# Attention outputs stored as half-precision pairs and turned by the reads of the last stage

## The chip, the cores and the metric

The kernel runs on one core of a Trainium2 chip. The core has a matrix engine (TensorE, PE in the rows), a vector engine (VectorE, DVE), an engine for activation functions and scaled copies (ScalarE, ACT), a general engine (GpSimd, POOL) and SyncE (SP), whose queue issues nearly all DMA transfers of this kernel. The engines run side by side, each through its own instructions in their order, and wait for each other on semaphores. The metric is the device time of one execution in microseconds (us), lower is better. Before the change it is 2896.48 us, the median of 3 runs from 2891.53 to 2901.36.

## What is computed

Two layers on 2048 tokens of width 1024: a Mamba-2 mixer, then multi-head latent attention with 16 heads, and a final RMS norm. The change lies in the end of the second layer, where `causal_block_attention` returns one 64-wide output per token and head:

```python
def mla_mixer(h, k_nope, k_rope, v, cos, sin, w_in, g_q, w_uq, w_out):
    ...
    o = causal_block_attention(q_nope, q_rope, k_nope, k_rope, v)
    o = o.reshape(Bsz, S, MLA_HEADS * V_HEAD) * jax.nn.silu(gate)
    return o @ w_out

h = h + mla_mixer(...)
return rms_norm(h, g_final)
```

## The kernel before

The program has three parts: `layers` (the Mamba layer and the projections for attention, up to about 1960 us), `attention` (to about 2705 us) and `back` (to the end). Results that cross the parts lie in device memory, among them the attention outputs `o_d` and the gates `gate_d`, both with 1024 channels as rows and 2048 tokens as columns.

**Attention.** A job is one head and one block of 512 queries (16 heads, 4 blocks, 64 jobs). Scores are made with keys on the partitions, two key tiles of 128 at a time (a duo); ACT takes the exponential into `x` (line 1371) and copies it to half precision as the high part of `PTs` (line 1376), POOL or DVE subtracts to get the low part (`lows`, line 1389), and PE multiplies the pair with the values (lines 1404 to 1406). The results of a job lie in one PSUM tile `o`, with queries on the partitions: [128, 4 tiles, 64 channels, and the row sum]. Row maxima for later jobs are taken by DVE from extra score products (lines 1252 and 1254), turned, stored in `m_d` and read back as rows (lines 1261 to 1270). On PE the order is the order of the code (`manual_schedule`); on the other engines and in SP's queue a scheduler orders by its own estimates.

When a job's last product is done, `finish` divides by the row sums: a reciprocal (line 1420) and a product into one half of the pair tile `Op` (line 1423), which holds two heads. After the odd head, three duos later (`TURN`), `store` has PE turn the four [128 queries, 128 channels] tiles into a score bank (line 1433), ACT copies the bank to `Os` (line 1435), and SP stores it in `o_d` (line 1437): 32 stores of 256 KB. The stores of heads 12 and 13 also start loads of the output weights (`load_wo`).

**Back.** The output projection runs over 4 blocks of 512 tokens, with 8 k-tiles of 128 channels each. `gated` makes the left operand of a k-tile: SP reads `o_d` into `os` and the gate beside it (lines 1519, 1520), DVE multiplies the two and a factor per channel (line 1521), and `split` makes a pair for float32 products (ACT line 107, DVE line 108). PE then runs 24 products per k-tile (`mm3`, lines 84 to 86). In the first block the loop goes k-tile by k-tile over 8 banks. Its k-tiles 0 and 1 are called early: they lie in `xT` buffers of a pool that lives through attention, so that their reads and products may run while attention still does. The others lie in a pool `bsp`, which opens when attention's pool `asp` closes; `os` has three buffers and the pairs `oT` have nine.

Of the kernel before, what the change touches and what calls it, by code (L numbers as in the profile page):

```python
# [10 lines left out]
F32 = mybir.dt.float32  # L11
F32R = mybir.dt.float32r
BF16 = mybir.dt.bfloat16
F16 = mybir.dt.float16
I32 = mybir.dt.int32
AF = mybir.ActivationFunctionType
ALU = mybir.AluOpType
# [50 lines left out]
class Net:  # L68
# [400 lines left out]
    def value_weights(self, owed):  # L469

        nc, v = self.nc, self.nc.vector
        for n in range(2):
            cs = slice(1024 + n * 512, 1536 + n * 512)
            raw = [self.t(self.wp, "wraw", [P, TB], bufs=WRAW) for _ in range(2)]
            for k in range(2):
                nc.sync.dma_start(raw[k], self.a["kv_w_up"][k * P:(k + 1) * P, cs])
            if owed:
                nc.sync.dma_start(*owed.pop())
            yield
            u = [self.t(self.wp, "wraw", [P, TB], F32R, bufs=WRAW) for _ in range(2)]  # L480
            for k in range(2):
                nc.scalar.activation(u[k], raw[k], AF.Abs, scale=self.gkl[:, k:k + 1])
            yield
            ps = self.t(self.pp, "tr", [P, TB], bufs=4)
            for k in range(2):
                nc.tensor.matmul(ps, self.ones_r, u[k], start=k == 0, stop=k == 1)
            x = self.t(self.sp, "cacc", [P, TB], bufs=2)
            v.tensor_scalar(x, ps, TINY, None, ALU.max)

            e = self.t(self.sp, "craw", [P, TB], I32, bufs=3)  # L490
            v.tensor_scalar(e, x.bitcast(I32), 23, None, ALU.logical_shift_right)
            f = self.t(self.sp, "cacc", [P, TB], I32, bufs=2)
            v.tensor_scalar(f, e, -1, 264, ALU.mult, ALU.add)
            v.tensor_scalar(f, f, 23, None, ALU.logical_shift_left)
            v.tensor_scalar(e[0:1], e[0:1], -25, None, ALU.add)
            v.tensor_scalar(e[0:1], e[0:1], 23, None, ALU.logical_shift_left)
            v.tensor_scalar(e[0:1].bitcast(F32), e[0:1].bitcast(F32), self.gdown[0:1], None, ALU.mult)
            nc.sync.dma_start(self.us_d[n * 512:(n + 1) * 512], e[0:1, :].bitcast(F32))
            for k in range(2):
                nc.gpsimd.tensor_tensor(raw[k], raw[k], f.bitcast(F32), ALU.mult)  # L500
            yield
            for k in range(2):
                w = self.t(self.wp, "wraw", [P, 2, TB], F16, bufs=WRAW)
                self.pair16(w[:, 0], w[:, 1], raw[k], self.gklv[:, k:k + 1])
                owed.append((self.wu_d[2 + n][k], w))
                yield
                nc.sync.dma_start(*owed.pop())
# [669 lines left out]
    def open_heads(self):  # L1177
# [9 lines left out]
        for i in range(2):  # L1187
            at = 2 * T + T // P * 130
            Q = self.quer[0, i] = kv[i][0:98, at:at + 2 * TB].rearrange("p (s t) -> p s t", s=2)
            self.fill_q(Q, 0, i)  # L1190
            nc.gpsimd.memset(self.keys[i][96:98, 0, :], MSCALE)
            nc.gpsimd.memset(self.vals[i][:, :, 128:130], 2.0 ** -14)
        self.load_k(0, 0, NB - 1)

    def load_vq(self):
# [109 lines left out]
    def heads(self, sp):  # L1305
# [109 lines left out]
        def finish(n):  # L1415

            h, qb = jobs[n]
            O = outs.pop(n)
            ri = self.t(sp, "ri", [P, 4], bufs=2)
            v.reciprocal(ri, O[:, :, 64])  # L1420
            if (h // 2, qb) not in pairs:
                pairs[h // 2, qb] = self.t(sp, "Op", [P, 4, 2, 64], bufs=6)
            v.tensor_tensor(pairs[h // 2, qb][:, :, h % 2, :], O[:, :, 0:64],
                            ri.unsqueeze(2).to_broadcast([P, 4, 64]), ALU.mult)
            if h % 2:
                later.append((step[0] + TURN, lambda: store(h, qb)))

        def store(h, qb):

            op = pairs.pop((h // 2, qb))  # L1430
            ps = bank()
            for j in range(4):
                nc.tensor.transpose(ps[:, j * P:(j + 1) * P], op[:, j].rearrange("p h d -> p (h d)"), self.ident)
            o = self.t(sp, "Os", [P, TB], bufs=2)
            act(o, ps, AF.Copy)
            r0 = (h // 2) * P
            done = nc.sync.dma_start(self.o_d[r0:r0 + P, qb * TB:(qb + 1) * TB], o)
            if h == NH - 3:
                with self.tc.issue_after(done.ins):
                    self.load_wo(qb)  # L1440
# [47 lines left out]
    def back(self):  # L1488
        nc, a, v, hp = self.nc, self.a, self.nc.vector, self.hp
        with ExitStack() as ctx:  # L1490
# [19 lines left out]
            def gated(b, k):  # L1510
# [5 lines left out]
                else:  # L1516
                    s = self.t(sp, "os", [P, 2, TB], bufs=3)
                o, gt = s[:, 0], s[:, 1]
                nc.sync.dma_start(o, self.o_d[rows, ts])
                nc.sync.dma_start(gt, self.gate_d[rows, ts])  # L1520
                v.scalar_tensor_tensor(o, o, us[:, k:k + 1], gt, ALU.mult, ALU.mult)
                u = self.t(self.xq, "xT", [P, 2, TB], F32R, bufs=8) if early else \
                    self.t(sp, "oT", [P, 2, TB], F32R, bufs=9)
# [76 lines left out]
    def run(self):  # L1600
        tc = self.tc
        with ExitStack() as whole:
# [5 lines left out]
            self.constants(cp)  # L1608
            self.h_d = dp.tile([T, D], F32, name="h_d")
            self.gate_d = dp.tile([D, T], F32, name="gate_d")  # L1610
            self.o_d = dp.tile([D, T], F32, name="o_d")
            self.xp_d = [dp.tile([TB, 2 * D], F16, name=f"xp{b}_d") for b in range(2 * NB)]
            self.m_d = dp.tile([NH * NB, P, 32], F16, name="m_d")
            self.qn_d = dp.tile([1024, 2, T], F16, name="qn_d")
# [70 lines left out]
```

## Time and profile before

The profiled execution took 2894.94 us, of which the span from the first to the last instruction is 2893.2 us.

| | us |
|---|---|
| median of 3 runs | 2896.48 |
| profiled execution | 2894.94 |
| its span | 2893.2 |
| PE busy in the span | 2809.5 (97%) |
| DVE, ACT, POOL busy | 2105.2, 1826.1, 854.8 |
| last product of attention starts at | 2704.05 |
| first product of `back` starts at | 2705.40 |

How to read it: the page lists busy time by engine, the busy shares in 40 slices, the chain of work that ended last (followed back from the last instruction, at each step to what released it), and groups of instructions with their mean durations and the idle time before them. Other views of the trace give the instructions in order of time, the waits by who waited for whom, and busy times by stretch. A row `x<-s` names the tile written and the tiles read. Products on PE overlap, so the distance from one start to the next is what one costs, and is less than the duration shown.

### The profile page before, as it was taken

To read this page: it belongs to the slowest core of one execution; us is meant where nothing else is said; L and a number is where in the kernel's file an instruction comes from. 1 tells how busy PE (TensorE), PEld (TensorE's weight loads), DVE (VectorE), ACT (ScalarE), POOL (GpSimd) and SP (SyncE) were. 2 spreads that over 40 slices of the span, in tenths; PEclk is the share of its full clock that TensorE was granted. 3 is DMA by queue.
4 is the path that set the end of the run, shared out by engine and by line. 5 is a ranking of instruction groups with operands and counts; after the bars stand their busy time and mean duration, and the time that the engine had idled before them with its cause. 6 is when DMAs were issued, how large, how long until landed. Compare 5 with 4: busy or idle time off the path is not lost.

```text
span 2893.2 us, 58394 instructions
## 1 busy us (share of the span) xinstructions
PE 2809.5 (97%) x21358; PEld 1643.2 (57%) x21358; DVE 2105.2 (73%) x5123; ACT 1826.1 (63%) x3948; POOL 854.8 (30%) x984
## 2 busy tenths in 40 slices
PE   7899999999999999999999999999999999999998
PEld 3455556554555555454555545545666666665787
DVE  7789987887777878779776455357777777778454
ACT  8777655666666766556554434234888888888522
POOL 0221221111222211222211122223666665665200
PEclk9999999999999999999999999999999999999999
DMA  9765736456464566636646877761222222223453
GB/s 294 248 208 193 215 118 215 149 171 192 146 237 132 176 192 218 212 117 214 209 138 233 252 227 230 235 206 59 72 55 63 64 51 74 67 64 89 166 198 109
DMA packets 308068, 470.77 MB, mean 163 GB/s; under 512 B 129474, under 2 KB 171234, under 8 KB 306340
## 3 DMA queue, kind: packets, MB, share of 16 engines
q1 hardware_dynamic: 296644, 431.11, 47.7%
q0 software_dynamic: 11136, 35.92, 3.4%
q8 instruction: 168, 2.75, 0.4%
q14 instruction: 120, 0.98, 0.1%
HBM read 332.83 MB, written 119.41 MB: 156 GB/s over the span
## 4 chain that ended last, share of the span: by engine, by line
PE 68%; DVE 16%; DMA 6%; ACT 5%; issue 4%; SPq 1%; POOL 1%; DVEq 0%; ACTq 0%; POOLq 0%
PE mm L84 11%; PE mm L85 11%; PE mm L86 11%; PE s L1365 4%; PE s L1366 4%; PE s L1367 4%; PE s L1252 4%; PE tr L85 3%; PE tr L84 3%; PE tr L86 3%; DVE cacc L647 3%; PE o L1405 2%; PE o L1406 2%; PE o L1404 2%; DMA big<-cumT 2%
## 5 line engine op out<-in xcount | busy, mean ns | idle before, releaser
L1389 POOL TENSOR_TENSOR PTs<-x,PTs 128x512 f16<-128x512 f32 (+1 forms) x380 | 439.2, 1179 | 264.6 <-ACT PTs L1376 173.6
L1371 ACT ACTIVATE x<-s 128x512 f32<-128x512 f32 (+3 forms) x640 | 326.9, 524 | 53.7 <-PE s L1367 34.6
L84 PE MATMUL mm<-xT,wsp 128*128 128x512 f16 x800 | 305.4, 382 | 6.1 <-ACT wsp L115 4.9
L85 PE MATMUL mm<-xT,wsp 128*128 128x512 f16 x800 | 304.9, 381 | 0.0
L86 PE MATMUL mm<-xT,wsp 128*128 128x512 f16 x800 | 304.4, 381 | 0.0
L1376 ACT ACTIVATE PTs<-x 128x1024 f16<-128x1024 f32 (+1 forms) x320 | 297.2, 929 | 9.4
L1254 DVE CUSTOM_DVE_ANT_0 junk<-s,fence,mx 128x512 bf16<-128x512 f32 (+1 forms) x372 | 242.1, 651 | 43.9 <-PE s L1252 3.8
L1406 PE MATMUL o<-K,PTs 128*128 128x65 f16 x2176 | 262.4, 192 | 2.0 <-POOL PTs L1389 1.5
L1404 PE MATMUL o<-K,PTs 128*128 128x64 f16 x2176 | 263.7, 192 | 0.1
L1405 PE MATMUL o<-K,PTs 128*128 128x65 f16 x2176 | 263.4, 194 | 0.0
L837 POOL TENSOR_TENSOR Xp<-Xw,Xp 128x512 fp32r<-128x512 f32 x64 | 90.5, 1414 | 504.1 <-ACT Xp L836 325.2
L1404 PEld LDWEIGHTS <-PTs 128*128 128x128 f16 x2176 | 204.6, 97 | 52.1 <-issue 4.3
L84 PE MATMUL mm<-wsp,xT 128*128 128x512 f16 (+1 forms) x640 | 230.5, 362 | 3.6 <-ACT craw L641 3.6
L85 PE MATMUL mm<-wsp,xT 128*128 128x512 f16 (+1 forms) x640 | 231.2, 361 | 2.1 <-DVE wsp L116 2.1
L1405 PEld LDWEIGHTS <-PTs 128*128 128x128 f16 x2176 | 202.7, 97 | 53.4 <-issue 1.0
L647 DVE SCALAR_TENSOR_TENSOR cacc<-craw,pack,cacc 128x512 f32<-128x512 f32 x288 | 215.5, 777 | 23.7 <-ACT cacc L645 22.3
L86 PE MATMUL mm<-wsp,xT 128*128 128x512 f16 (+1 forms) x640 | 231.1, 361 | 0.0
L1365 PE MATMUL s<-xT,K 98*128 98x512 f16 (+1 forms) x628 | 219.0, 349 | 3.7 <-DVE mx L1254 3.7
L1252 PE MATMUL s<-K,xT 96*128 96x512 f16 (+1 forms) x616 | 214.0, 349 | 5.6 <-DVE mx L1254 4.0
L1366 PE MATMUL s<-xT,K 96*128 96x512 f16 (+1 forms) x628 | 218.8, 348 | 0.0
L1367 PE MATMUL s<-xT,K 96*128 96x512 f16 (+1 forms) x628 | 217.2, 346 | 0.0
L84 PE MATMUL mm<-wsp,yT 128*128 128x512 f16 (+1 forms) x512 | 197.8, 386 | 7.9 <-DVE sz L671 6.3
(475 smaller groups left out, 7179.9 us busy)
## 6 DMA issues: line engine op xcount, KB each, us to landing
wsp<-wi_d SPq DMA_DIRECT2D x96, 512.0 KB
big<-cumT SPq DMA_DIRECT2D x64, 512.0 KB
wraw<-in_ssm_w_out_dram SPq DMA_DIRECT2D x96, 256.0 KB
wi_d<-wsp SPq DMA_DIRECT2D x32, 512.0 KB
wsp<-wo_d SPq DMA_DIRECT2D x32, 512.0 KB
wsp<-wu_d SPq DMA_DIRECT2D x28, 512.0 KB
hx<-in_ssm_w_in_dram SPq DMA_DIRECT2D x48, 256.0 KB
wraw<-in_ssm_w_in_dram SPq DMA_DIRECT2D x48, 256.0 KB
```

The source lines that it names most:

```text
L84: mm(out, l_hi, r_hi, start=start, stop=False)
L85: mm(out, l_hi, r_lo, start=False, stop=False)
L86: mm(out, l_lo, r_hi, start=False, stop=stop)
L1252: self.nc.tensor.matmul(s[:, :w], Q[0:96], K[0:96], start=True, stop=True)
L1365: mm(s, K[0:98, 0, ks], Q[0:98, 0, c], start=True, stop=False)
L1366: mm(s, K[0:96, 0, ks], Q[0:96, 1, c], start=False, stop=False)
L1367: mm(s, K[0:96, 1, ks], Q[0:96, 0, c], start=False, stop=kb < 4 * qb)
L1371: act(o, s, AF.Exp)
L1389: engine.tensor_tensor(u[:, 1, a:b], x[:, a:b], u[:, 0, a:b], ALU.subtract)
L1404: mm(o[:, 0:64], hi, V[:, k, 0:64], start=k == 0 and j == 0, stop=False, skip_group_check=True)
L1405: mm(o[:, 0:65], hi, V[:, k, 64:129], start=False, stop=False, skip_group_check=True)
L1406: mm(o[:, 0:65], lo, V[:, k, 64:129], start=False, stop=k == 4 * qb + j, skip_group_check=True)
```

## The change

`finish` writes the quotient to a tile `On`, copies it on ACT to half precision as the high part, and has POOL subtract that to get the low part. The pair tile `Op` has the same bytes as before but holds [4 tiles, high or low, 128 channels of two heads] in half precision. `store` issues one transfer from it as it lies, with tokens as rows, into one of four tensors `o_d[qb]`; the four turns on PE and the copy out of the bank are gone. `gated` reads the pair by a transposing DMA into a new tile `oz` (three buffers, pool `bsp`), and POOL adds the two parts into the tile that was loaded before. Two constants change with the scale of the values (2^-14 to 1, and -25 to -11 in an exponent).

```diff
-            v.tensor_scalar(e[0:1], e[0:1], -25, None, ALU.add)
+            v.tensor_scalar(e[0:1], e[0:1], -11, None, ALU.add)
...
-            nc.gpsimd.memset(self.vals[i][:, :, 128:130], 2.0 ** -14)
+            nc.gpsimd.memset(self.vals[i][:, :, 128:130], 1.0)
...
             if (h // 2, qb) not in pairs:
-                pairs[h // 2, qb] = self.t(sp, "Op", [P, 4, 2, 64], bufs=6)
-            v.tensor_tensor(pairs[h // 2, qb][:, :, h % 2, :], O[:, :, 0:64],
-                            ri.unsqueeze(2).to_broadcast([P, 4, 64]), ALU.mult)
+                pairs[h // 2, qb] = self.t(sp, "Op", [P, 4, 2, P], F16, bufs=6)
+            o = self.t(sp, "On", [P, 4, 64], bufs=3)
+            v.tensor_tensor(o, O[:, :, 0:64], ri.unsqueeze(2).to_broadcast([P, 4, 64]), ALU.mult)
+            hi, lo = (pairs[h // 2, qb][:, :, m, h % 2 * 64:(h % 2 + 1) * 64] for m in range(2))
+            act(hi, o, AF.Copy)
+            nc.gpsimd.tensor_tensor(lo, o, hi, ALU.subtract)
...
         def store(h, qb):
-            op = pairs.pop((h // 2, qb))
-            ps = bank()
-            for j in range(4):
-                nc.tensor.transpose(ps[:, j * P:(j + 1) * P], op[:, j].rearrange("p h d -> p (h d)"), self.ident)
-            o = self.t(sp, "Os", [P, TB], bufs=2)
-            act(o, ps, AF.Copy)
-            r0 = (h // 2) * P
-            done = nc.sync.dma_start(self.o_d[r0:r0 + P, qb * TB:(qb + 1) * TB], o)
+            op, c0 = pairs.pop((h // 2, qb)), (h // 2) * 2 * P
+            done = nc.sync.dma_start(self.o_d[qb][:, c0:c0 + 2 * P].rearrange("(j p) c -> p j c", p=P),
+                                     op.rearrange("p j m c -> p j (m c)"))
...
-                nc.sync.dma_start(o, self.o_d[rows, ts])
+                z = self.t(sp, "oz", [P, 2, TB], F16, bufs=3)
+                nc.sync.dma_start_transpose(z, self.o_d[b][:, 2 * k * P:2 * (k + 1) * P])
                 nc.sync.dma_start(gt, self.gate_d[rows, ts])
+                nc.gpsimd.tensor_tensor(o, z[:, 0], z[:, 1], ALU.add)
...
-            self.o_d = dp.tile([D, T], F32, name="o_d")
+            self.o_d = [dp.tile([TB, 2 * D], F16, name=f"o{b}_d") for b in range(NB)]
```

Three places show what this moves. The first is SP's queue in the last heads of attention, before the change: `m_d<-rT` and `xT<-m_d` are the way of the row maxima, `wr` the output weights, and the reads of `xT` from `o_d` and `gate_d` are those of k-tile 1 of the first block of `back`.

```order
L1226 DMA wr_37022<-in_mla_w_out_dram 128x1024
L1264 DMA m_d<-rT_35515 128x32
L1519 DMA xT_37059<-o_d 128x512
L1520 DMA xT_37059<-gate_d 128x512
L1270 DMA xT_34736<-m_d 1x16x32 x2
```

The same place with the change:

```order
L1226 DMA wr_37030<-in_mla_w_out_dram 128x1024
L1264 DMA m_d<-rT_35493 128x32
L1226 DMA wr_37068<-in_mla_w_out_dram 128x1024
L1270 DMA xT_34726<-m_d 1x16x32 x2
L1226 DMA wr_37108<-in_mla_w_out_dram 128x1024
```

The reads of the attention outputs for k-tiles 0 and 1 have left this place; of the four early reads only the gate of k-tile 0 stays in attention. The second place is SP's queue where attention ends, before the change (the last four stores, then `os` for k-tiles 2 and 3):

```order
L1437 DMA o_d<-Os_36850 128x512
L1437 DMA o_d<-Os_36997 128x512
L1519 DMA os_37095<-o_d 128x512
L1520 DMA os_37095<-gate_d 128x512
L1561 DMA gf<-in_g_final_dram 128x1024
L1519 DMA os_37133<-o_d 128x512
L1520 DMA os_37133<-gate_d 128x512
```

And with the change, where `oz_36996`, `oz_37033` and `oz_37071` are the turned reads of k-tiles 0, 1 and 2, and `xT_37032` is the gate of k-tile 1:

```order
L1434 DMA o_d<-Op_35862 128x4x256
L1434 DMA o_d<-Op_36236 128x4x256
L1518 DMA_TRANSPOSE oz_36996<-o_d 128x2x512
L1518 DMA_TRANSPOSE oz_37033<-o_d 128x2x512
L1518 DMA_TRANSPOSE oz_37071<-o_d 128x2x512
L1519 DMA os_37070<-gate_d 128x512
L1561 DMA gf<-in_g_final_dram 128x1024
L1519 DMA xT_37032<-gate_d 128x512
L1518 DMA_TRANSPOSE oz_37111<-o_d 128x2x512
L1519 DMA os_37110<-gate_d 128x512
```

All turned reads, also those of the two early k-tiles, now stand behind the last store of attention, because `oz` lies in `bsp`. The third place is ACT where attention ends, with the change (`K` takes the high part of output weights, lines 1505 before and 1503 after):

```order
L1376 ACTIVATE PTs_36870<-x_36869 128x384
L1503 ACTIVATE K_7069_37215<-wr_37068 128x2x512
L1426 ACTIVATE Op_36236<-On_36966 128x4x64
L1503 ACTIVATE K_7069_37215<-wr_37108 128x2x512
L107 ACTIVATE xT_37001<-xT_36995 128x512
L107 ACTIVATE oT_37076<-os_37070 128x512
```

The last copy to half precision stands behind one of the weight copies, and the `split` of k-tile 0 (line 107) now follows here; before, it stood among the exponentials of heads 14 and 15.

## The prediction

> **What bounds the kernel now.** I read the page first, then busy times by stretch, then the chain of waits inside attention, and last the order of time where attention ends.
>
> ```profile
> span 2893.2 us, 58394 instructions
> PE 2809.5 (97%) x21358; PEld 1643.2 (57%) x21358; DVE 2105.2 (73%) x5123; ACT 1826.1 (63%) x3948; POOL 854.8 (30%) x984
> ```
>
> PE is busy 97% of the span, so what counts is PE time taken away or PE made to wait. The instructions of the layers before attention are not touched. Inside attention, one stretch of four heads, and the chain over the steady part:
>
> ```profile
> 2166.90:2343.00 176.10, 175.57 (x2367) 116.60 (x2366) 135.06 (x399) 155.14 (x264) 111.22 (x112) 1.00 0.26 63
> by line: PE s L1365 16.2%; PE s L1366 16.1%; PE s L1252 15.9%; PE s L1367 15.9%; PE o L1405 9.2%; PE o L1406 9.0%; PE o L1404 8.8%; PE s L1369 2.0%; PE s L1433 2.0%; DVE junk L1254 1.7%; issue 1.0%; ACT PTs L1376 0.9%; ACT x L1371 0.6%; ACT
> ```
>
> The first row gives, after the length, busy us of PE, weight loads, DVE, ACT and POOL, then the granted clock and the DMA share. PE is full, ACT 88%, DVE 77%, POOL 63%. The second is the chain from 1990 to 2600 us: nearly all of it is PE products, and 2.0% of it are the turns of line 1433 that the change takes out. So in steady attention a turn removed is time won, as long as ACT's 12% of room holds.
>
> **Removed: the turns on PE.** The duration shown for one turn is not its price:
>
> ```profile
> L1433 PE MATMUL s<-pack,Op x128: 272/273/328, 2049.5 to 2705.4; 128*128 128x128 f32 x128
> 2089.51 0.47 PE s L1433 x4
> ```
>
> 128 times 273 ns would be 34.9 us, but the turns overlap: four take 0.47 us of the chain of waits. 32 stores by 0.47 us are 15.0 us. Of these 2.0% of 610 us, 12.2 us or 26 stores, lie in the steady part. Six are left, after 2600 us; the first and last of those on the chain before the end, and a stretch among the last duos:
>
> ```profile
> 2603.73 0.47 PE s L1433 x4
> ...
> 2697.35 0.47 PE s L1433 x4
> 2680.00:2700.00 20.00, 20.00 (x300) 13.85 (x299) 7.68 (x14) 19.68 (x33) 14.90 (x11) 1.00 0.08 28
> ```
>
> I count 0.5 us for the one at 2603, none for one in the stretch that DVE sets (below), and half, 0.7 us, for three among the last duos, where ACT, 19.68 of 20 us, fills its time as PE does; the last store belongs to the gap below. Together **-13.4 us**.
>
> **Added in attention: copies on ACT, subtractions on POOL.** No row has these exact shapes (128x256), so the nearest bound them:
>
> ```profile
> L1435 ACT ACTIVATE Os<-s 128x512 f32<-128x512 f32 x31 | 17.9, 578 | 0.0
> L1371 ACT ACTIVATE x<-s 128x256 f32<-128x256 f32 x63 | 23.0, 366 | 0.0
> L1376 ACT ACTIVATE PTs<-x 128x384 f16<-128x384 f32 x64 | 33.5, 523 | 2.0
> L1389 POOL TENSOR_TENSOR PTs<-x,PTs 128x512 f16<-128x512 f32 x374 | 433.4, 1182 | 263.7 <-ACT PTs L1376 172.7 <-issue 63.6 <-POOL PTs L1389 10.2
> L1389 POOL TENSOR_TENSOR PTs<-x,PTs 128x128 f16<-128x128 f32 x3 | 1.6, 544 | 0.0
> ```
>
> A copy costs ACT 0.37 to 0.52 us; I take 0.40. 64 of them are 25.6 us, and 32 copies out of the bank by 0.578 us, 18.5 us, go: ACT gains 7 us over 700 and stays under PE, 89% to 91% busy. A subtraction costs POOL 0.54 to 1.18 us; I take 0.75, near the middle of widths: 48 us over 700, which lifts POOL from 63% to 70%. What can cost something is order: behind the copy stand the exponentials that free PE's score banks, and behind the subtraction the low parts of `PTs`, for which PE's value products wait, and the small subtraction of the row maxima (line 1262), for which DVE waits. Six score banks and three held duos cover a wait of about a microsecond. I price this at **+1.5 us**, a PE wait of 0.2 us at each of the eight pairs of heads, between -1 (a store no longer takes a score bank) and 4 (0.5 us, a whole copy, at each pair). The store itself is one SP issue for another, of the same bytes.
>
> **Moved: the early k-tiles of `back`.** The reads of the attention outputs for k-tiles 0 and 1 no longer run during heads 14 and 15. What their products cost there:
>
> ```profile
> L1506 DVE TENSOR_TENSOR W<-wr,W 128x1024 fp32r<-128x1024 f32 x4 | 5.6, 1396 | 1.1 <-ACT W L1505 1.1
> L1521 DVE SCALAR_TENSOR_TENSOR xT<-xT,us 128x512 f32<-128x512 f32 x2 | 2.6, 1298 | 1.5 <-issue 1.5
> L108 DVE TENSOR_TENSOR xT<-xT,xT 128x512 fp32r<-128x512 f32 x2 | 2.1, 1030 | 0.0
> 2560.00:2580.00 20.00, 20.00 (x292) 13.89 (x290) 17.19 (x49) 17.15 (x32) 8.93 (x10) 1.00 0.41 94
> 2610.00:2630.00 20.00, 17.78 (x226) 11.37 (x225) 16.04 (x42) 16.35 (x30) 7.77 (x8) 1.00 0.61 166
> 2630.00:2650.00 20.00, 16.97 (x186) 9.91 (x185) 19.08 (x44) 16.49 (x27) 14.47 (x11) 0.91 0.33 108
> ```
>
> Where a stretch before has PE busy all 20 us, the next two miss 2.2 and 3.0 us, and the clock of 0.91 takes 1.8 us more: 7.0 us lost. DVE has extra work here, 5.6 us for output weights, which stays, and 2.6 + 2.1 us plus 1.5 us of waiting for a read, 6.2 us, which leaves. By its share of the extra work, 6.2 of 11.8, that gives 3.7 us back; I take **-4 us**, between 0 (the weights alone hold PE as long) and 7.
>
> **Added: a gap where `back` begins.** Here the cover is gone. The end of attention before:
>
> ```profile
> 2704.05 0.20 PE L1406 MATMUL o<-K,PTs 128*128 128x65 f16 x1
> 2704.29 2.01 ACT L1505 ACTIVATE K<-wr 128x1024 fp32r<-128x1024 f32 x2 [1.42 <-PE o L1406]
> 2704.51 0.42 DVE L1423 TENSOR_TENSOR Op<-o,ri 128x256 f32<-128x256 f32 x1
> 2705.40 0.48 PE L84 MATMUL mm<-K,xT 128*128 128x512 f32 x1
> 2706.81 0.32 SPq L1437 DMA_DIRECT2D o_d<-Os  x1
> 2716.51 0.40 PE L84 MATMUL mm<-W,oT 128*128 128x512 f32 x1
> ```
>
> PE goes on at 2705.40 with k-tiles that are ready, 11.1 us for two, 5.55 us each, and only k-tile 2 has to be read meanwhile. With the change k-tile 0 itself is read behind the last store. The prices of that way, beside the rows above:
>
> ```profile
> 714.60 3.53 SPq L619 DMA_TRANSPOSE xT<-xp_d  x2
> 719.38 0.59 PE L764 MATMUL tr<-xT,wdt 128*64 128x512 f16 x2 [0.24 <-DMA xT<-xp_d]
> 720.25 0.59 PE L764 MATMUL tr<-xT,wdt 128*64 128x512 f16 x2 [0.27 <-DMA xT<-xp_d]
> 332.00:338.00 6.00, 6.00 (x32) 3.02 (x30) 6.00 (x11) 2.57 (x4) 2.21 (x2) 1.00 0.94 199
> L837 POOL TENSOR_TENSOR Xp<-Xw,Xp 128x512 fp32r<-128x512 f32 x64 | 90.5, 1414 | 504.1 <-ACT Xp L836 325.2 <-issue 128.5 <-PE tr L843 20.2
> L1521 DVE SCALAR_TENSOR_TENSOR os<-os,us x30: 746/752/756, 2711.9 to 2834.6; 128x512 f32<-128x512 f32 x30
> 2712.70 0.63 ACT L107 ACTIVATE oT<-os 128x512 fp32r<-128x512 f32 x1 [5.92 <-DVE os L1521]
> ```
>
> The layers read their inputs by the same kind of transfer in the same shape: PE waited for two, and the first had landed 4.8 us after its issue began, the second 0.9 us later. On the clock of before: the quotient is done at 2704.93; ACT is in the first of two weight copies until 2705.30, then the copy, 2705.70; subtraction 2706.45; store issued to 2706.85; the turned read begins and lands 4.8 us later, 2711.65; POOL's sum, between 1.18 and 1.41 us by the two rows of that width, 1.3, to 2712.95; DVE 0.75, ACT 0.63, with some 0.1 us of hand-overs: PE starts at 2714.5 in place of 2705.40. **+9.1 us**, between 8.4 (a landing as of the second read) and 12 (a landing of 7.7 us, below). Behind it k-tiles 1 and 2 are read at once, POOL's sums for them end at 2714.25 and 2715.55, and DVE takes the order 0, 2, 1: k-tile 2's product and low part to 2717.65 (0.75 + 0.63 + 0.7 us), then k-tile 1's product to 2718.4 and ACT to 2719.05, 4.5 us after k-tile 0 and inside the 5.55 us that PE spends on it.
>
> The idle stretch has a second price, the clock. The granted clock after a stretch in which PE had little to do:
>
> ```profile
> 106.60:110.10 3.50, 0.97 (x3) 0.48 (x3) 2.24 (x3) 3.14 (x11) 2.30 (x3) 0.99 1.01 334
> 110.10:113.50 3.40, 1.46 (x4) 0.59 (x5) 3.04 (x7) 3.40 (x7) 0.00 (x0) 0.50 0.68 179
> 113.50:116.90 3.40, 3.40 (x10) 1.22 (x8) 3.40 (x7) 3.40 (x7) 0.64 (x2) 0.50 0.89 217
> 1099.90:1103.30 3.40, 3.32 (x14) 3.27 (x15) 2.38 (x9) 1.65 (x6) 0.00 (x0) 0.50 0.73 218
> ```
>
> After the long gap two stretches of 3.4 us ran at half clock, 4.86 us of them busy, which costs half of that, 2.4 us; after a short gap it was one, 1.7 us. The new gap, about 10 us, is like the long one: **+2.4 us**, between 1.7 and 3.4.
>
> Here a rule can be weighed. In the window at 332 us, where nearly all traffic is turned reads, the DMA engines are 94% busy at 199 GB/s, 1.3 us for 256 KB. The Trainium skill, "Advanced Engine Details and Errata", X-Bar Transpose (TRN2), says that such transfers are as fast as regular ones and expects 350 to 400 GB/s, by an estimate 0.7 us. The trace does not agree; by the page the first read would land 0.6 us earlier and the sum would be 0.6 us lower.
>
> **The sum.** -13.4 + 1.5 - 4 + 9.1 + 2.4 = -4.4 us. Against the profiled execution's 2894.94 us that is 2890.5 us. The median of the runs, 2896.48, is 1.5 us above that execution, so the predicted time is **2892 us**, 0.15% less. About 0.3%, 8.7 us, is what a measurement of this kernel can tell from no change.
>
> **The rivals.** *The gap is cheap and heads 14 and 15 recover fully.* For it: DVE has 19.08 of 20 us in the window at 2630, so all 7 us may be its doing. Against it: the weight copies stay. With -13.4, 0, -7, 8.4 and 1.7 it is -10.3 us, 2886 us.
>
> *Attention does not shrink.* If copies and subtractions make ACT or POOL late at every job, the 13.4 us are eaten: -4 + 9.1 + 2.4 = +7.5 us, 2904 us. For it: ACT at 88%, and each copy waits for DVE. Against it: ACT's work grows by only 1% and it has 12% of room.
>
> *The turned reads set the pace of the first block of `back`; slower than before.* Its place is the eight k-tiles after the gap. Three buffers `oz` and `os` each, SP in order, a read behind a gate that waits for a buffer: a k-tile may come later than PE uses one up. In the chain of before the longest piece there is
>
> ```profile
> 2723.77 7.74 DMA os<-gate_d
> ```
>
> A k-tile each 7.74 us in place of 5.55 us makes seven waits of 2.2 us, 15 us, and -4.4 + 15 = +11 us, 2907 us. It decides at 5.55 us a k-tile. Against it: turned reads followed each other at 0.9 to 1.3 us above, and with three in flight a round of 4.8 + 1.4 + 2.1 us (read, sum, DVE and ACT) gives one each 2.8 us.
>
> A rule goes further this way. The Trainium skill, "VectorE: DVE Perf Modes", The three transpose paths, gives 1309 ns for one 128x128 turn by DMA against 390 ns on TensorE, and its rules prefer TensorE. Taken one after another, eight turns make 10.5 us a read by an estimate. The rows above, two reads 0.9 us apart, do not agree.
>
> As a mechanism, reads that cannot overlap at all cost their whole 4.8 us and the 1.4 us of the sum after it, 6.2 us a k-tile: seven waits of 0.65 us, 4.5 us, and no change in sum, 2896 us.
>
> **How the numbers follow.** The forecast has 0.54, the cheap gap 0.22, attention not shrinking 0.10, the pace of the reads 0.12, reads without overlap 0.02. Faster by over 0.3% (below 2887.8) is the cheap gap, 0.22. Slower by over 0.3% (above 2905.2) is the pace, 0.12. The rest, 0.66, is within. The range goes from 2884, the cheap gap with 2 us of scatter, to 2904, attention not shrinking; with the terms at their dear ends, -13.4 + 4 + 0 + 12 + 3.4 = +6, the sum stays inside.
>
> **What would show it.** Line 1433 gone, and steady attention about 1.9 us shorter per two heads (four turns of 0.47 us); if not, ACT or POOL rows stand in the chain there. PE idle for about 10 us before the first product on `xT` of `back`, waiting for DVE, ACT and at last the turned read `oz`, then one or two stretches at half clock. PE fuller between 2600 and 2650 us, with no line 1521 among the heads. After the gap no PE wait for `os` or `oT`. The prediction is wrong if the first read starts before the last store, if it lands much later than 4.8 us, or if PE waits at each k-tile.

## The result, and the profile after

The changed kernel takes **2938.18 us**, the median of 4 runs from 2932.55 to 2940.91, against 2896.41 us for the kernel before in the same comparison: a ratio of 1.0146, with a 95% interval from 1.0133 to 1.0159. It is slower by 42 us, where 2892 us had been forecast. The profiled execution took 2940.91 us. Two lines of its page, span and busy time:

```profile
span 2939.1 us, 58313 instructions
PE 2810.7 (96%) x21230; PEld 1631.7 (56%) x21230; DVE 2116.6 (72%) x5123; ACT 1826.3 (62%) x3980; POOL 932.2 (32%) x1080
```

PE is busy only 1.2 us longer than before, so of the 45.9 us added to the span nearly all is time in which PE stands idle. The span is cut at two landmarks, the first reciprocal of attention (line 1420) and the start of attention's last product:

| stage | before | after | difference |
|---|---|---|---|
| layers | 2000.0 | 2002.8 | +2.8 |
| attention | 704.1 | 724.6 | +20.5 |
| last stage | 189.1 | 211.7 | +22.6 |

The layers run the same instructions in all kernels here, and yet end between 1996.2 and 2005.3 us. A single time carries that scatter, so the experiments below are read by stage.

The busy times by stretch for the changed kernel (columns as in the prediction: length, PE, weight loads, DVE, ACT, POOL, granted clock, DMA share, GB/s), first in steady attention, then where the stages meet:

```profile
2166.90:2343.00 176.10, 168.63 (x2268) 109.71 (x2267) 131.05 (x384) 149.85 (x265) 115.25 (x124) 1.00 0.26 62
...
2720.00:2740.00 20.00, 9.17 (x136) 7.16 (x133) 8.19 (x12) 9.06 (x15) 12.07 (x9) 0.77 0.42 114
2740.00:2760.00 20.00, 20.00 (x86) 16.26 (x86) 12.96 (x14) 4.42 (x7) 6.10 (x5) 0.97 1.03 245
2760.00:2780.00 20.00, 20.00 (x88) 16.22 (x87) 12.43 (x13) 3.95 (x7) 8.53 (x7) 1.00 1.03 204
2780.00:2800.00 20.00, 10.17 (x33) 7.77 (x32) 9.25 (x16) 5.43 (x11) 4.79 (x4) 0.74 0.68 147
```

PE was full in the first stretch before, 175.57 us; now 7.5 us of it are empty, spread over four heads. And there are two holes near the end, one at the start of the last stage and one some 50 us later. The chain through steady attention, 1990 to 2600 us, by line:

```profile
by line: DVE junk L1254 17.5%; issue 10.5%; PE s L1252 8.6%; PE s L1365 8.5%; PE s L1366 7.5%; ACT x L1371 7.5%; PE s L1367 7.4%; POOL PTs L1389 4.4%; DVE PTs L1389 4.3%; PE o L1405 4.3%; PE o L1406 4.2%; PE o L1404 4.1%; ACT PTs L1376 3.0%
```

It was nearly all PE before. Now it runs over DVE's row maxima (line 1254), ACT's exponentials and POOL's low parts: the engines take turns in being late.

**Where attention loses.** The same pattern returns at every head of the steady part, mostly to within a few hundredths of a microsecond. Here it is in order of time (start, length, engine, instruction, and in brackets the idle time before it and what ended it), at the third block of queries of one head, in the kernel before. The first two rows are from the same place one head earlier:

```profile
2205.88 0.08 DVE L1254 DVE_READ_ACCUMULATOR2_ANT mx<- 128x1 f32 x1
2206.14 0.38 PE L1365 MATMUL s<-xT,K 98*128 98x512 f16 x1
...
2242.13 6.82 POOL L1389 TENSOR_TENSOR PTs<-x,PTs 128x512 f16<-128x512 f32 x6 [0.19 <-POOL PTs L1389]
2246.89 0.08 DVE L1254 DVE_READ_ACCUMULATOR2_ANT mx<- 128x1 f32 x1
2248.91 0.20 POOL L1262 TENSOR_TENSOR nm<-mx,nm 128x4 f16<-128x4 f32 x1
2249.15 0.21 DVE L1263 STREAM_TRANSPOSE rT<-nm 128x32 f16<-128x32 f16 x1 [2.17 <-POOL nm L1262]
2249.88 0.09 DVE L1254 DVE_READ_ACCUMULATOR2_ANT mx<- 128x1 f32 x1
2250.09 0.63 PE L1433 MATMUL s<-pack,Op 128*128 128x128 f32 x4
2250.55 0.22 PE L1252 MATMUL s<-K,xT 96*128 96x128 f16 x1
```

And the same place in the changed kernel:

```profile
2255.81 0.42 DVE L1424 TENSOR_TENSOR On<-o,ri 128x256 f32<-128x256 f32 x1
2256.27 0.42 ACT L1426 ACTIVATE Op<-On 128x256 f16<-128x256 f32 x1 [1.01 <-DVE On L1424]
2257.63 0.66 POOL L1427 TENSOR_TENSOR Op<-On,Op 128x256 f16<-128x256 f32 x1
2257.69 1.06 ACT L1376 ACTIVATE PTs<-x 128x1024 f16<-128x1024 f32 x1
2258.56 0.08 DVE L1254 DVE_READ_ACCUMULATOR2_ANT mx<- 128x1 f32 x1
2258.82 2.28 POOL L1389 TENSOR_TENSOR PTs<-x,PTs 128x512 f16<-128x512 f32 x2 [0.53 <-ACT PTs L1376]
2261.06 0.20 POOL L1262 TENSOR_TENSOR nm<-mx,nm 128x4 f16<-128x4 f32 x1
2261.29 0.21 DVE L1263 STREAM_TRANSPOSE rT<-nm 128x32 f16<-128x32 f16 x1 [2.65 <-POOL nm L1262]
2262.03 0.08 DVE L1254 DVE_READ_ACCUMULATOR2_ANT mx<- 128x1 f32 x1
2262.17 0.38 PE L1365 MATMUL s<-xT,K 98*128 98x512 f16 x1 [0.91 <-DVE mx L1254]
```

Read it from the top. ACT comes to the copy of line 1426 and stands for 1.01 us, because DVE has the quotient behind a row of maxima. With the copy itself ACT is 1.4 us late for the exponentials, its `PTs` (line 1376) ends at 2258.75, and POOL, which waited 0.53 us for it, starts two low parts of 2.28 us together. Behind them stands the small subtraction of the row maxima, `nm`, and for that DVE waits 2.65 us. In that time no maximum is taken, the bank that PE needs next does not come free, and PE stands for 0.91 us.

Before, POOL ran six low parts through without a wait for ACT, and DVE stood 2.17 us: **a wait that cost PE nothing but left it little cover.** The cover can be read in the rows as the time from the end of the maximum that frees a bank to the product of PE that takes it. One head earlier it is 0.18 us, from 2205.96 to 2206.14. At the place shown it is 0.58 us, from 2249.97 to 2250.55, and 0.46 of these are the four turns, which the change takes out. So without the turns some 0.1 to 0.2 us are left, and DVE waits half a microsecond longer.

**Where the last stage loses.** Its start in the changed kernel:

```profile
2727.43 0.20 PE L1406 MATMUL o<-K,PTs 128*128 128x65 f16 x1
2728.64 0.40 ACT L1426 ACTIVATE Op<-On 128x256 f16<-128x256 f32 x1
2728.76 2.83 DVE L1504 TENSOR_TENSOR K<-wr,K 128x1024 fp32r<-128x1024 f32 x2 [0.45 <-ACT K L1503]
2729.11 1.40 POOL L1427 TENSOR_TENSOR Op<-On,Op 128x256 f16<-128x256 f32 x1 [1.74 <-ACT Op L1426]
2730.54 0.37 SPq L1434 DMA_DIRECT2D o_d<-Op  x1
2731.01 4.01 SPq L1518 DMA_TRANSPOSE oz<-o_d  x3
2734.32 1.15 POOL L1520 TENSOR_TENSOR xT<-oz 128x512 f32<-128x512 f16 x1 [3.81 <-DMA oz<-o_d]
2735.51 0.75 DVE L1521 SCALAR_TENSOR_TENSOR xT<-xT,us 128x512 f32<-128x512 f32 x1 [3.91 <-POOL xT L1520]
2736.29 0.63 ACT L107 ACTIVATE xT<-xT 128x512 fp32r<-128x512 f32 x1 [6.31 <-DVE xT L1521]
2736.97 0.79 PE L84 MATMUL mm<-K,xT 128*128 128x512 f32 x1 [9.34 <-ACT xT L107]
```

This is the forecast gap, step by step: 9.54 us from the last product to the first, 1.35 before, so +8.2. The second hole was not forecast. PE and DVE at the change from the first to the second block, and the clock behind both holes:

```profile
2782.66 0.75 DVE L1521 SCALAR_TENSOR_TENSOR os<-os,us 128x512 f32<-128x512 f32 x1 [2.34 <-DMA os<-gate_d]
2783.17 0.40 PE L86 MATMUL tr<-K,oT 128*128 128x512 f32 x1
2786.22 0.75 DVE L1521 SCALAR_TENSOR_TENSOR os<-os,us 128x512 f32<-128x512 f32 x1 [2.80 <-POOL os L1520]
2791.30 0.75 DVE L1521 SCALAR_TENSOR_TENSOR os<-os,us 128x512 f32<-128x512 f32 x1 [3.73 <-DMA os<-gate_d]
2792.57 2.47 DVE L1536 TENSOR_TENSOR h<-h,mm 128x512 f32<-128x512 f32 x4
2793.40 0.76 PE L84 MATMUL mm<-K,oT 128*128 128x512 f32 x1 [9.83 <-DVE h L1536]
...
2730.80:2741.00 10.20, 4.03 (x9) 3.01 (x10) 3.16 (x4) 1.12 (x2) 4.23 (x3) 0.50 0.89 217
2788.90:2799.10 10.20, 5.70 (x14) 4.47 (x15) 6.79 (x11) 3.42 (x7) 1.16 (x1) 0.50 0.46 102
```

PE ended the first block at 2783.17 and had all eight banks full. DVE empties them (line 1536), but in its order three more left operands of later k-tiles come first, and they wait for a gate, for POOL's sum of a turned read, and for a gate again (these are queued on SP behind turned reads). PE waits 10.23 us from start to start; before it was 0.79. The half clock costs half of the busy time in it: 2.0 us behind the first hole, 2.9 us behind the second. So the last stage's 22.6 us are 8.2 + 2.0 + 9.4 + 2.9, within 0.1 us.

### The profile page after: what moved, and what is told of

Read it like the earlier page. It is cut to its first block, busy times and chain, and to the rows that moved or that the text cites. A ratio compares the mean times of both kernels' runs of the same rounds, so it can differ in the third digit from the quotient of the medians.

```text
span 2939.1 us, 58313 instructions
## 1 busy us (share of the span) xinstructions
PE 2810.7 (96%) x21230; PEld 1631.7 (56%) x21230; DVE 2116.6 (72%) x5123; ACT 1826.3 (62%) x3980; POOL 932.2 (32%) x1080
## 4 chain that ended last, share of the span: by engine, by line
PE 59%; DVE 20%; ACT 7%; DMA 6%; issue 5%; POOL 2%; SPq 1%; DVEq 0%; ACTq 0%; POOLq 0%
PE mm L84 11%; PE mm L86 11%; PE mm L85 11%; DVE junk L1254 4%; PE tr L85 4%; PE tr L84 4%; PE tr L86 4%; DVE cacc L647 3%; PE s L1365 2%; PE s L1252 2%; PE s L1366 2%; PE s L1367 2%; ACT x L1371 2%; DMA big<-cumT 2%; PE tr L914 2%
## 5 line engine op out<-in xcount | busy, mean ns | idle before, releaser
L1371 ACT ACTIVATE x<-s 128x512 f32<-128x512 f32 (+3 forms) x640 | 320.4, 523 | 51.7 <-PE s L1367 27.2
```

Of the source, the lines that this page charges most:

```text
L1371: act(o, s, AF.Exp)
```

## The experiments

A pair of heads has eight reciprocals of line 1420. Its time is measured from the 9th to the 49th of them, divided by five: 88.37 us before, 91.37 after. It repeats to 0.03 us wherever attention is the same. In the first four runs the kernel before took 2899.32 us beside them, in e5 to e8 2899.84, in e9 to e12 2896.18.

**Attention and last stage apart.** In e1 attention is as changed, and the last stage reads plain rows, the gates in place of the attention outputs:

```diff
-                z = self.t(sp, "oz", [P, 2, TB], F16, bufs=3)
-                nc.sync.dma_start_transpose(z, self.o_d[b][:, 2 * k * P:2 * (k + 1) * P])
+                nc.sync.dma_start(o, self.gate_d[rows, ts])
                 nc.sync.dma_start(gt, self.gate_d[rows, ts])
-                nc.gpsimd.tensor_tensor(o, z[:, 0], z[:, 1], ALU.add)
```

> The attention part of the change alone; the last stage reads its gate tile a second time in place of the attention outputs (plain reads, early for k-tiles 0 and 1, as before the change), so its output leaves attention out. If the loss of the change is made of two separate parts, attention takes 91.3 us per pair of heads as in the changed kernel (88.4 before), the gap at the start of the last stage is about 1.4 us as before, no stall of 10 us stands at the change of blocks, and the time is about 2896 + 21 = 2917 us. If the slow attention comes from the last stage (its reads, its tiles), the pair of heads takes 86.5 to 88.4 us and the time is below 2900 us.

e2 is the other half: attention as before, the turned reads in the last stage, of data of the same shape:

```diff
-                nc.sync.dma_start(o, self.o_d[rows, ts])
+                z = self.t(sp, "oz", [P, 2, TB], F16, bufs=3)
+                nc.sync.dma_start_transpose(z, self.xp_d[NB + b][:, 2 * k * P:2 * (k + 1) * P])
                 nc.sync.dma_start(gt, self.gate_d[rows, ts])
+                nc.gpsimd.tensor_tensor(o, z[:, 0], z[:, 1], ALU.add)
```

> The last-stage part alone: attention as before the change, while the last stage reads turned tiles of the layer inputs (same shape and type, other data), so its output leaves attention out. If the parts are separate: 88.4 us per pair of heads, a gap of 8 to 11 us before the last stage's first product, a stall of about 10 us where the first block changes to the second, together 2896 + 8 + 2 + 12 = 2918 us. If the stall at the change of blocks needs the slow attention, only the gap is there: 2906 us.

e1 took 2919.78 us, a pair of heads 91.34: the loss of attention needs nothing from the last stage. Its last stage takes 192.0 us and has one wait of 2.6 us for an operand in place of the holes. e2 took 2908.38 us, less than the 2918 expected of separate parts, though both holes are there (9.63 and 9.54 us). Its last stage is 209.7 us, 20.6 more than before, and its attention 699.1 us, 5.0 less: the early k-tile work that left heads 14 and 15.

**Which engine.** e3 makes the copy on VectorE, e6 the subtraction, e7 both:

```diff
-            act(hi, o, AF.Copy)
-            nc.gpsimd.tensor_tensor(lo, o, hi, ALU.subtract)
+            v.tensor_copy(hi, o)                       # e3, e7
+            v.tensor_tensor(lo, o, hi, ALU.subtract)   # e6, e7
```

> The changed kernel with the copy to half precision on DVE in place of ACT, behind the quotient on the same engine. Theory A (ACT stands at the copy until DVE has made the quotient, 34.7 us in all, and the exponentials behind it free PE's banks late): the pair of heads falls from 91.3 to 88 us or less and the time from 2938 to about 2912 us. Theory B (the subtraction on POOL delays the row maxima's subtraction and so DVE): it stays at 90.5 us or more, since POOL has the same work, and DVE has 0.3 us more per job.

> The subtraction of the high part goes to VectorE, the copy stays with ScalarE. Theory 'GpSimd's 694 ns subtraction, which waits for ScalarE's copy, stands in front of the small subtraction of the row maxima (nm) that VectorE and then TensorE wait for': VectorE's waits for nm fall from 96 us to below 80 in the stretch 2010 to 2600, a pair of heads takes 87 to 89 us, the kernel 2920 to 2930. Theory 'VectorE itself is the late one': it gets 64 operations more that wait for ScalarE in its own order, so a pair of heads takes 91.5 to 94 and the kernel 2940 to 2960.

> Copy and subtraction both on VectorE, one behind the other; ScalarE and GpSimd have nothing of the pair. Theory 'the detour over two other engines is the cost': no engine waits for another inside the pair, a pair of heads takes 87 to 89 us, the kernel 2918 to 2930. Theory 'VectorE's time in front of the maxima is the cost': some 0.42 + 0.4 us more for each of 8 outputs of a pair of heads, a pair of heads 91 to 95, the kernel 2938 to 2965.

None helps: 2940.29, 2937.64 and 2945.28 us, a pair of heads 91.96, 91.49 and 92.63. The theory that it is enough to spare ACT its wait falls with e3. e6 shows that the way over POOL is not the only one: from 2100 to 2600 us DVE waits 58.5 us for `nm`, less than the 66.5 of the kernel before, and PE still waits 17.4 us for maxima. All three edits put the work on DVE, which takes the maxima, so they do not tell what each operation costs; the next two runs do.

**Neither of the two, and one of them.** e5 writes the quotient at once in half precision and stores it in both places; e18 keeps ACT's copy and leaves out POOL's subtraction:

```diff
-            act(hi, o, AF.Copy)
-            nc.gpsimd.tensor_tensor(lo, o, hi, ALU.subtract)
+            act(pairs[h // 2, qb][:, :, h % 2 * 64:(h % 2 + 1) * 64], o, AF.Copy)   # e18 only
...
+            for m in range(2):
+                done = nc.sync.dma_start(
+                    self.o_d[qb][:, c0 + m * P:c0 + (m + 1) * P].rearrange("(j p) c -> p j c", p=P), op)
```

> Stands beside the changed kernel: VectorE writes the product at once in half precision into the pair's tile, and the store writes it twice, in both halves' places; ScalarE's 64 copies and GpSimd's 64 subtractions are left out (the outputs' low parts are wrong). The turns on TensorE are gone as in the changed kernel. Theory 'the copies and subtractions stand in front of the row maxima': without them attention is bounded by TensorE again, a pair of heads takes 86.5 us (the forecast's figure) and the kernel some 20 to 30 us less than the changed one, 2908 to 2918. Theory 'taking the turns out of TensorE's order sets the waits, whatever stands in their place': a pair of heads stays at 89.5 to 91.3 and the time at 2930 to 2940.

> The changed kernel with GpSimd's 64 subtractions left out and ScalarE's 64 copies kept where they are; the store writes the high parts twice (the outputs' low parts are wrong). If the wait of ScalarE for On is the cost: a pair of heads stays at 90 to 91.4 us, the kernel 2924 to 2940. If the subtraction in front of the maxima is: a pair of heads 86.8 to 88, the kernel 2896 to 2908. Between, 88 to 90 us and 2908 to 2924: each costs a part.

e5 took 2896.43 us, e18 2936.26 (2891.95 for the kernel before beside it). The reciprocals of e5 in a window of one pair of heads, nine of them, so that the last starts one pair after the first:

```profile
L1420 DVE RECIPROCAL ri<-o x9: 177/177/180, 2182.4 to 2269.2; 128x4 f32<-128x4 f32 x9
```

A pair of heads takes 86.83 us without the two operations, 91.10 with the copy, 91.37 with both. **The copy on ACT costs 4.27 of the 4.54 us, and the subtraction on POOL, added to it, 0.27**, though it is the longer one (694 ns against 413). What the subtraction costs without the copy was not run. In e18, at the place shown above:

```profile
2257.25 0.42 ACT L1425 ACTIVATE Op<-On 128x256 f16<-128x256 f32 x1 [1.01 <-DVE On L1424]
2259.81 2.27 POOL L1389 TENSOR_TENSOR PTs<-x,PTs 128x512 f16<-128x512 f32 x2 [1.16 <-ACT PTs L1376]
2262.27 0.21 DVE L1263 STREAM_TRANSPOSE rT<-nm 128x32 f16<-128x32 f16 x1 [2.64 <-POOL nm L1262]
```

The subtraction's 0.66 us have only turned into POOL's longer wait for ACT, and DVE's wait is the same to 0.01 us.

**The wait, the place, the way of the maxima.** e4 makes copy and subtraction at the store, three duos later, for two heads at once; e10 one duo later, each output by itself (with a fourth buffer for `On`); e12 is e4 with the subtraction on VectorE:

```diff
+            op = self.t(sp, "Op", [P, 4, 2, P], F16, bufs=2)                    # e4, e12: in store
+            act(op[:, :, 0], on, AF.Copy)
+            nc.gpsimd.tensor_tensor(op[:, :, 1], on, op[:, :, 0], ALU.subtract)  # e12: v
...
+            later.append((step[0] + 1, split))    # e10: split has the two lines of finish
```

> The changed kernel with copy and subtraction made at the store, three duos after the odd head's quotient, 128x512 each, on the same engines. If waits are the loss (A or B, an engine standing for a result that is not there yet), nothing waits any more and the pair of heads takes 86.5 to 88 us, the time falls to about 2905 to 2912 us. If the added work itself is the loss (POOL 44 us more), it stays above 90 us and 2930 us.

> The copy and the subtraction of each output as in the changed kernel (128x256 each, ScalarE and GpSimd), but put into the program one duo of blocks later, so that On has long been written when ScalarE comes to the copy. If ScalarE's wait for On (24.2 us of 500) is what costs: that wait goes, a pair of heads 87 to 88.5 us, the kernel 2912 to 2922. If it is the place of the work among the exponentials and in front of nm: the wait goes too, but a pair of heads stays above 89.5 and the kernel at 2922 to 2942.

> As the pair made late (copy at the store, 128x512 on ScalarE), with the subtraction of 128x512 on VectorE, so that GpSimd has none of it. The pair made late took 2918.0 us with 89.7 us for a pair of heads. If GpSimd's place in front of nm is what is left there: 87 to 88.5 us and 2900 to 2910. If VectorE's time counts as much: 89.5 to 91.5 and 2917 to 2932.

e9 leaves the pair as it is and takes the maxima off the two other engines:

```diff
-        nc.scalar.activation(u[:, 0:4], e, AF.Copy)
-        nc.gpsimd.tensor_tensor(u[:, 4:8], e, u[:, 0:4], ALU.subtract)
+        nc.vector.tensor_copy(u[:, 0:4], e)
+        nc.vector.tensor_tensor(u[:, 4:8], e, u[:, 0:4], ALU.subtract)
```

> The changed kernel with one edit far from the pair: the two small operations of 128x4 that split a block's row maxima (nm; 0.20 us on ScalarE, 0.21 us on GpSimd in the changed kernel) go to VectorE, which turns them next, so VectorE waits for no other engine there; the pair's copy and subtraction stay where they are. Theory 'the pair's work stands in front of nm on ScalarE and GpSimd, VectorE waits there (81.5 us of 500), the next maxima are late and TensorE runs out of score banks': VectorE's waits for nm go, a pair of heads takes 87 to 88.5 us instead of 91.3, the kernel 2912 to 2922. Theory 'it is VectorE's own load, or ScalarE's head-of-line wait for On': VectorE gets 128 small operations more, a pair of heads 91 to 93, the kernel 2936 to 2955.

| run | us | pair of heads |
|---|---|---|
| e4 | 2918.0 | 89.62 |
| e10 | 2924.16 | 90.20 |
| e12 | 2912.71 | 88.90 |
| e9 | 2921.1 | 89.73 |

Each takes away a part, and none reaches the 87 to 88.5 us a pair that were expected if one wait were the whole cause. With the copy made late the subtraction counts more: taken off POOL, it gives 0.72 us a pair (e4 to e12). Three rows of the waits in the changed kernel from 2100 to 2600 us (us in total, times, longest), and the row for ACT's copy in e10:

```profile
DVE rT L1263 <- POOL nm L1262: 81.5, 44, 2.6
ACT Op L1426 <- DVE On L1424: 24.2, 33, 1.0
PE s L1365 <- DVE mx L1254: 16.5, 33, 0.9
```

```profile
ACT Op L1429 <- DVE On L1424: 14.7, 22, 0.9
```

One duo is not late enough: 39% of ACT's 24.2 us of waiting went, and 1.17 of the 4.54 us of a pair. e9 shows that the way over the maxima is a link of the chain: without it a pair loses 1.64 us less, though ACT waits more for `On` than in the changed kernel:

```profile
ACT Op L1426 <- DVE On L1424: 43.5, 44, 1.4
```

**The two holes.** e8 gives the turned reads of the two early k-tiles a place in the pool that lives through attention:

```diff
-                z = self.t(sp, "oz", [P, 2, TB], F16, bufs=3)
+                z = self.t(self.xq, "xT", [P, 2, TB], F16, bufs=8) if early else \
+                    self.t(sp, "oz", [P, 2, TB], F16, bufs=3)
```

> The changed kernel with one edit: the tiles of the turned reads of the first two blocks of rows of the last stage come from the pool that is free during attention, as the sums' tiles do, so that these reads need not wait for the pool of the last stage. The forecast's account of the gap at the start of the last stage (8.2 us of empty TensorE and some 2 us of half clock): the gap falls to 1 to 2 us and the kernel by 6 to 10 us, 2928 to 2932; less if the work on these tiles goes back in front of heads 14 and 15 (the last product of attention then comes 4 to 7 us later than in the changed kernel). Rival 'the gap is a wait for the store of the last head or the port': gap 8 to 10 us as before, kernel 2936 to 2941.

e11 puts the left operands of k-tiles 4 to 7 behind the residuals of the block before:

```diff
+                with self.tc.issue_after(done.ins):     # done: the last residual
+                    oT += [gated(b, k) for k in range(4, 6)]
                 final(b - 1, hs, 0)
-                oT += [gated(b, k) for k in range(6, KD)]
+                with self.tc.issue_after(done.ins):
+                    oT += [gated(b, k) for k in range(6, KD)]
```

> The changed kernel with one edit in the last stage: the left operands of k-tiles 4 to 7 of each block are put behind the residuals that empty the banks of the block before, on VectorE, where the changed kernel has all eight of the next block and two of the one after ahead of them. If VectorE's order is what makes the gap of 10.2 us at the change from the first to the second block: the gap falls to 2 to 4 us, the half clock behind it goes too, and the kernel gains 7 to 11 us, 2927 to 2932; the same products may then wait later, for the operands that were put back. If the turned reads simply cannot bring the operands faster: the gap shrinks but the wait comes back in the second block, and the kernel stays at 2936 to 2942.

In e8 (2925.45 us) the first gap is 0.04 us and the last stage 195.7 us, 16.0 shorter; attention is 2.4 longer, with the early work back in it. The second hole shrank too, to 6.7 us: DVE's order has two operands fewer ahead of the residuals. In e11 (2930.99 us) the second hole is gone and the last stage is 12.1 us shorter, 199.6; DVE stands ready when PE ends:

```profile
2780.86 2.77 DVE L1536 TENSOR_TENSOR h<-h,mm 128x512 f32<-128x512 f32 x4 [5.03 <-PE mm L86]
2783.66 2.77 DVE L1536 TENSOR_TENSOR h<-h,tr 128x512 f32<-128x512 f32 x4
```

and from 2740 us on PE waits for no operand longer than 0.5 us:

```profile
PE mm L86 <- DVE oT L108: 0.5, 1, 0.5
```

So the turned reads do keep PE's pace once DVE's order is mended. The order alone does not make the hole: in e8 DVE has 16 left operands in front of the first residual, as many as in the kernel before (18 in the changed kernel, 12 in e11), and PE waits 6.7 us with turned reads where it waited 0.79 with plain ones. It takes both, slower reads and an order in which the residuals stand behind them.

**All three places at once.** e13 has the edits of e8, e11 and e12. e14 has e9's and e4's in place of e12's; e15 has all four; e16 is the kernel before with e9's edit alone. e17 is e13 again, timed by 11 runs of it and 15 of the kernel before.

> The pair made late with the subtraction on VectorE (e12, 2912.7 us), and the two mends of the last stage in the same kernel: the first turned reads kept early (e8) and the residuals ahead (e11). If the three places are the whole of the loss and add up: 8 to 10 us less for the start and 8 to 10 less for the change of blocks, with the early work back in front of the last heads (4 to 7 us more): 2896 to 2903. If the turned reads' rate bounds the last stage in any order: one gap comes back elsewhere, 2904 to 2912.

> As e13, but the pair's subtraction on GpSimd again and the maxima kept on VectorE (e9) in its place. If the wait for the maxima on GpSimd is one and the same that e12 took away: the same time as e13 within 4 us. If GpSimd's subtraction costs at other places too: 4 us slower or more.

> All mends together: pair late, subtraction and maxima on VectorE, early reads early, residuals ahead. If the mends of attention add up: a pair of heads 87 to 88 us (e12 88.9, e9 1.7 less than the changed kernel) and 5 to 12 us less than e13, below the kernel before, 2884 to 2895. If they take the same wait away, or VectorE (some 400 and 450 us busy of 500 in e12 and e9) becomes the bound: as e13 or slower.

> The kernel before with the maxima's split on VectorE and nothing else. There TensorE is busy for 498.7 of 500 us, so there is no wait to take away: 88.4 us for a pair of heads as it is, 2894 to 2899. If VectorE's place is tight there too: slower, 2900 to 2915.

> The kernel of e13 again, timed in rounds against the kernel before. If the three places are the whole of the 42 us and the mends take them away, the ratio lies between 0.998 and 1.002. If something of the loss lies elsewhere, above 1.002.

e13 took 2896.58 us, e14 2906.81, e16 2892.96, against a median of 2895.68 for the kernel before; e15 2900.67, ratio 1.0016 (1.0005 to 1.0027). e17 took 2899.49 us against 2896.47, **ratio 1.0010 (1.0001 to 1.0019)**: of the 42 us some 3 are left, and the change with its three places mended is no faster than the kernel before. Its last stage takes 188.5 us, as before, its attention 706.5, 2.4 more than before at 88.91 us a pair. The mends of attention do not add up: with e9's edit on top, e15 has 89.39, where e12 alone has 88.90; DVE is busy there for 452.0 of 500 us (373.4 in the changed kernel), and what holds PE then was not tried further. e16's 88.23 us a pair show that in the kernel before there is almost nothing to gain there.

## Why the prediction was wrong

**The turns, -13.4 us: right.** e2 and e5 both lack the early work, and differ in attention by the turns and their copies: 699.1 and 686.8 us, -12.3. That is 1.54 us a pair of heads, where 1.9 was named.

**Copies and subtractions, +1.5 us: this is the step that failed.** Attention is 724.6 us with them and 686.8 without (e5): +37.8 us. The durations were right, 413 ns where 0.40 us was taken and 694 ns where 0.75 was. What failed is the sentence that six score banks and three held duos cover a wait of about a microsecond. The rows of before show 0.18 us of cover at one head and 0.58 at the next, most of that the turns themselves, so the first term of the sum took away cover that the second one counted on. With the turns gone and no pair work (e5), PE waits 2.8 us for maxima from 2100 to 2600 us, against 1.3 before and 20.3 in the changed kernel. The prediction took the cover as free because PE was never idle; the trace of before had already shown DVE standing 2.17 us in front of the maxima, a wait that drew on that same cover. The price was then set by busy shares, ACT at 88%, and the upper end, a whole copy at each pair of heads, was too low by its form: PE waits three times at every head, by about 0.4, 0.9 and 0.4 us. The prediction's own sign of this, ACT and POOL rows in the chain of steady attention, came. Of the 4.54 us a pair, 4.27 are the copy's. How these divide between ACT's wait for `On` and the 0.4 us of the copy itself stays open: where the wait was smaller (e4, e10), the copy was also in another place.

**The rival that attention does not shrink** named the mechanism, a copy that waits for DVE, but capped its price at the gain of 13.4 us. Nothing in the profile gave that cap.

**Early work, -4 us: right.** -5.0 in e2, 2.4 between e8 and the changed kernel.

**The gap, +9.1, and its clock, +2.4: right in mechanism and nearly in size,** 8.2 and 2.0. Some of the closeness is luck: the first read landed 3.3 us after its issue began, where 4.8 was taken, and POOL's subtraction took 1.40 us, where 0.75 was taken.

**The second hole, +12.3 us: a term that the sum did not have.** The working followed three k-tiles behind the gap and stopped at a k-tile's operands in time for PE. The rival on the pace of the reads looked at these operands as well, and so at the wrong place: PE was full through the block, 20.00 of 20 us from 2740 to 2780, and stood at its end for its banks. Its rule of thumb, that a wait decides above 5.55 us a k-tile, does not apply to residuals that stand behind late operands in DVE's order, which e8 and e11 showed to be the cause.

The terms as measured, -12.3 + 37.8 - 5.0 + 8.2 + 2.0 + 12.3, make 43.0 us, against 43.1 us for attention and last stage together. The first three are steps from one run to the next and add up to attention's 20.5 us by construction; the last three are read from rows.

On the rate of turned reads, the Trainium skill, "Advanced Engine Details and Errata", X-Bar Transpose (TRN2), expects 350 to 400 GB/s. From 2740 to 2780 us the changed kernel's DMA engines are busy all the time, share 1.03, at 245 and 204 GB/s, with turned reads and gates mixed; the trace does not agree here either.

## What to carry to other kernels

A bound engine that never waits doesn't show how much cover is left in front of it. Read the time from the moment a buffer comes free to the moment the bound engine takes it, subtract the work that the change removes in between, and only then set an added wait against it. The price of an added operation does not follow its length: here a copy of 413 ns cost sixteen times what a subtraction of 694 ns cost on top of it. When a read becomes slower, look in each engine's order for what stands behind its consumers, and not only at the consumers.

## What the runs showed of the hardware

Turned reads fill the DMA engines at a lower rate than plain ones: share 1.03 at 204 to 245 GB/s in the rows above. The kernel before, over its first block of the last stage, with plain reads of the same outputs and gates:

```profile
2720.00:2740.00 20.00, 20.00 (x88) 16.21 (x87) 9.81 (x15) 4.43 (x7) 0.00 (x0) 1.00 0.84 282
```

And subtractions on POOL and DVE lengthen each other. Of POOL's 64 subtractions of 128x256 (line 1427) 61 take 0.66 to 0.68 us. The other three start while DVE is in a subtraction of its own, and take 0.86, 1.16 and 1.40 us; the last is the one at 2729.11 us above. The other way round, DVE's low part of 128x896 takes 1.09 us at most when it has no such neighbour, and 1.40 when it starts within POOL's subtraction, as happens once at each of 14 heads of the changed kernel:

```profile
2233.82 1.40 DVE L1389 TENSOR_TENSOR PTs<-x,PTs 128x896 f16<-128x896 f32 x1
```

In e18, without POOL's subtraction, none of the 61 takes longer than 1.09 us; in the changed kernel 14 do. The Trainium skill, "SBUF — State Buffer", Who interferes with whom, says that a VectorE operation with two inputs in SBUF contends with a GpSimd operation that reads SBUF. The rows of the changed kernel and of e18 agree.
